# A rotary embedding kernel: the first row of slab 1 moved to ScalarE's DMA ring at the start

## The chip, the cores and the metric

The kernel runs on one core of a Trainium2 chip. The metric is the device time of one execution in microseconds (us), smaller being better. The five engines of the core run their own instruction streams: TensorE (PE), VectorE (DVE), ScalarE (ACT), GpSimd (POOL) and SyncE (SP). Data moves between the main memory and the on-chip memory by 16 DMA engines. A DMA is issued by SyncE, ScalarE or GpSimd, each into a ring of its own, and the 16 DMA engines serve all the rings.

## The reference

Rotary position embedding, in float32, over x of shape (16, 512, 1024), seen as 16 heads of 64. The two halves of each head are rotated by the cosine and sine of the position:

```python
x = x.reshape(batch, seq, num_heads, head_dim)
x1, x2 = x[..., :half_dim], x[..., half_dim:]
cos = cos[None, :, None, :]
sin = sin[None, :, None, :]
rotated = np.concatenate([
    x1 * cos - x2 * sin,
    x1 * sin + x2 * cos
], axis=-1)
```

The output has 16 x 512 x 16 x 64 float32 values: 33.55 MB are read and 33.55 MB written.

## The kernel before

The input is cut into 8 slabs (`nslabs`) of two batches each. A slab is a tile of 128 partitions x 8192 float32 (`W`), 4 MB: each partition holds 8 rows (`rpp`) of 1024 elements (`dim`), which lie side by side in the main memory, so that one partition is one run of 32 KB. There are five slots for slabs (`slots`), and a slab is written back from the slot it was loaded into.

Loads are issued by SyncE, one DMA for each slab (`load`, L60 to L62). Load 0 is the first DMA. Then GpSimd issues the loads of the cosine and the sine table (L73, into `raw`). Loads 1 to 4 carry a dependency written out by hand on the cosine table (L80): SyncE issues them once that table has landed. Loads 5, 6 and 7 are issued inside the loop (L150) and wait until the store of the slab that held their slot has landed.

The tables are spread to all rows by GpSimd (L89 to L98, a selection matrix `pick` and a bf16 copy of the tables) and eight small matmuls (L104), and VectorE copies the result into `tab` (L110). This happens once.

The work on the slabs goes in passes. The first slab and the last two are done in two passes of four rows each, the others in one pass of eight. For each pass ScalarE casts the slab to bf16 (`cast`, L119, into `xb`), VectorE does two multiplications (L140) and one addition (L143), and ScalarE casts the result back into the slab (L146). After the last pass of a slab ScalarE issues the store (L148). ScalarE's program order is: the cast of pass 0, then for each pass the cast of the next pass, the copy back of this pass, and the store. So the stores and all work of ScalarE stand in one program order, and before the change the first DMA that ScalarE issues is the store of slab 0.

Of the kernel before, what the change touches and what calls it, by code (L numbers as in the profile page):

```python
# [2 lines left out]

# [4 lines left out]


@with_exitstack  # L10
def kernel(
    ctx: ExitStack,
    tc: tile.TileContext,
    x: bass.AP,
    cos: bass.AP,
    sin: bass.AP,
    num_heads: int,
    out: bass.AP,
):
    nc = tc.nc  # L20
    P = nc.NUM_PARTITIONS

    batch, seq, dim = x.shape
    nh = num_heads
    hd = dim // nh
    half = hd // 2
    bf16 = mybir.dt.bfloat16
    f32 = mybir.dt.float32

    nb = 2  # L30
    slots = 5
    nslabs = batch // nb
    rpp = nb * seq // P
    W = rpp * dim
    SP = seq // rpp
    TW = rpp * half

    out_flat = out.rearrange("b s h d -> b s (h d)")

    singles = ctx.enter_context(tc.tile_pool(name="singles", bufs=1))  # L40
    slabs = ctx.enter_context(tc.tile_pool(name="slabs", bufs=slots))
    xpool = ctx.enter_context(tc.tile_pool(name="xpool", bufs=2))
    psum = ctx.enter_context(tc.tile_pool(
        name="psum", bufs=1, space=bass.MemoryType.PSUM))


    def dram(t, s, a=0, n=W):
        return bass.AP(tensor=t.tensor, offset=t.offset + s * nb * seq * dim + a,
                       ap=[[W, P], [1, n]])


    def view(t, offset, *dims):
        return dataclasses.replace(t, offset=t.offset + offset,
                                   ap=[t.ap[0], *[list(d) for d in dims]])


    slab = {}


    def load(s):  # L60
        slab[s] = slabs.tile([P, W], f32, tag="slab", name="slab")
        return nc.sync.dma_start(out=slab[s], in_=dram(x, s))  # L62


    load(0)


    TR = seq // P
    G = rpp // TR
    table = {}  # L70
    raw = singles.tile([P, 2 * TR * half], f32, tag="raw")
    for i, src in enumerate((cos, sin)):
        table[i] = nc.gpsimd.dma_start(out=view(raw, i * TR * half, (1, TR * half)), in_=bass.AP(  # L73
            tensor=src.tensor, offset=src.offset,
            ap=[[TR * half, P], [1, TR * half]]))

    for s in range(1, slots):
        tc.add_manual_dep(  # L80
            load(s).ins, table[0].ins.name,
            mybir.DependencyInfo(mybir.DependencyClass.Sync,
                                 mybir.DependencyReason.DATA),
            reason="issue")

    pick = singles.tile([P, 2 * G * P], bf16, tag="pick")
    nc.gpsimd.memset(pick, 0.0)  # L89
    for g in range(2 * G):  # L90
        part = view(pick, g * P, (SP, P // SP), (1, SP))
        nc.gpsimd.affine_select(  # L92
            out=part, in_=part, compare_op=mybir.AluOpType.not_equal,
            fill=1.0 if g < G else -1.0, base=-(g % G),
            pattern=[[0, P // SP], [-G, SP]], channel_multiplier=1)

    tab1 = singles.tile([P, 2 * TR * half], bf16, tag="tab1")
    nc.gpsimd.tensor_copy(out=tab1, in_=raw)  # L98

    acc = psum.tile([P, 2 * rpp * hd], f32, tag="acc")  # L100
    for i in range(2):
        for h in range(2):
            for g in range(G):
                nc.tensor.matmul(  # L104
                    view(acc, (i * rpp + g * TR) * hd + h * half, (hd, TR), (1, half)),
                    view(pick, (i * h * G + g) * P, (1, P)),
                    view(tab1, i * TR * half, (half, TR), (1, half)),
                    start=True, stop=True)
    tab = singles.tile([P, 2 * rpp * hd], bf16, tag="tab")
    nc.vector.tensor_copy(out=tab, in_=acc)  # L110

    xb = {}


    def cast(u):
        s, r, n = u
        if r == 0:
            xb[s] = xpool.tile([P, W], bf16, tag="xb", name="xb")
        nc.scalar.copy(out=view(xb[s], r * dim, (1, n * dim)),  # L119
                       in_=view(slab[s], r * dim, (1, n * dim)))  # L120

    passes = []
    for s in range(nslabs):
        n = rpp if 1 <= s < nslabs - 2 else rpp // 2
        passes += [(s, r, n) for r in range(0, rpp, n)]


    cast(passes[0])
    for i, (s, r, n) in enumerate(passes):
        if i + 1 < len(passes):
            cast(passes[i + 1])
        xs = view(slab[s], r * dim, (1, n * dim))
        xu = view(xb[s], r * dim, (1, n * dim))

        t2 = view(slab[s].bitcast(bf16), 2 * r * dim, (1, n * dim))
        for t, a in ((t2, rpp * hd), (xu, 0)):
            nc.vector.tensor_mul(  # L140
                out=t, in0=xu,
                in1=view(tab, a + r * hd, (hd, n), (0, nh), (1, hd)))
        nc.vector.tensor_add(  # L143
            out=xu, in0=xu, in1=view(t2, half, (hd, n * nh), (-half, 2), (1, half)))

        nc.scalar.copy(out=xs, in_=xu)  # L146
        if r + n == rpp:
            nc.scalar.dma_start(out=dram(out_flat, s), in_=slab[s])  # L148
            if s + slots < nslabs:
                load(s + slots)  # L150


# [1 line left out]
_INS = ['x', 'cos', 'sin', 'num_heads']  # L154
_OUTS = [((16, 512, 16, 64), 'float32')]

_NUMBERS = {'num_heads': 16}


# [26 lines left out]
```

## Time and profile before

| What | Value |
|---|---|
| Median of 4 runs | 162.28 us (162.18 to 162.3) |
| The profiled execution: its time | 162.27 us |
| The profiled execution: its span, first to last instruction | 160.5 us |
| ScalarE busy | 113.5 us (71%) |
| VectorE busy | 108.5 us (68%) |
| Data moved | 67.24 MB, 419 GB/s over the span |
| Issue of load 0 (SyncE) | 0.74 us |
| Cosine and sine table, issue to landing | 7.2 and 9.1 us |
| First cast (slab 0) / cast of slab 1 start | 13.50 / 23.20 us |
| First store issued (ScalarE) | 37.26 us |
| Last store issued (ScalarE) | 144.66 us |

The table reads in order of time: the span counts from the first instruction, and the time of the execution holds 1.8 us around it. In the views, L140 is line 140 of the kernel, `slab<-xb` is a tile that is written and what is read for it, and ACTq or SPq is the queue of an engine that issues DMAs. A DMA ring appears as q1 (SyncE's), q10 (ScalarE's) and q0 (GpSimd's). The granted clock was 1.0 in the whole execution.

### The profile page before, as it was taken

To read this page: it belongs to the slowest core of one execution; us is meant where nothing else is said; L and a number is where in the kernel's file an instruction comes from. 1 tells how busy PE (TensorE), PEld (TensorE's weight loads), DVE (VectorE), ACT (ScalarE), POOL (GpSimd) and SP (SyncE) were. 2 spreads that over 40 slices of the span, in tenths; PEclk is the share of its full clock that TensorE was granted. 3 is DMA by queue.
4 is the path that set the end of the run, shared out by engine and by line. 5 is a ranking of instruction groups with operands and counts; after the bars stand their busy time and mean duration, and the time that the engine had idled before them with its cause. 6 is when DMAs were issued, how large, how long until landed. Compare 5 with 4: busy or idle time off the path is not lost.

```text
span 160.5 us, 169 instructions
## 1 busy us (share of the span) xinstructions
PE 1.0 (1%) x8; PEld 0.8 (1%) x8; DVE 108.5 (68%) x34; ACT 113.5 (71%) x23; POOL 3.4 (2%) x12
## 2 busy tenths in 40 slices
PE   0011000000000000000000000000000000000000
PEld 0010000000000000000000000000000000000000
DVE  0003799999989979997996199939559599910000
ACT  3006939998998999899909995099995999280000
POOL 7000000000000000000000000000000000000000
DMA  7999999999999999999999999999999999999994
GB/s 245 425 408 392 465 449 392 441 474 392 351 433 400 465 441 392 474 441 392 474 441 392 449 449 408 425 465 416 416 457 433 400 466 441 392 474 441 392 474 180
DMA packets 2368, 67.24 MB, mean 419 GB/s; under 512 B 288, under 2 KB 288, under 8 KB 320
## 3 DMA queue, kind: packets, MB, share of 16 engines
q1 hardware_dynamic: 1152, 33.55, 49.5%
q10 hardware_dynamic: 1152, 33.55, 48.4%
q0 software_dynamic: 64, 0.13, 0.2%
HBM read 33.69 MB, written 33.55 MB: 419 GB/s over the span
## 4 chain that ended last, share of the span: by engine, by line
DMA 49%; ACT 30%; issue 6%; DVE 4%; ACTq 0%; SPq 0%; POOLq 0%
DMA slab<-in_x_dram 24%; DMA out_dram<-slab 21%; ACT slab L146 16%; ACT xb L119 14%; DMA raw<-in_cos_dram 4%; DVE slab L140 1%; DVE xb L140 1%; DVE xb L143 1%; ACTq L148 0%; SPq L62 0%; ACTq L146 0%; POOLq L167 0%
## 5 line engine op out<-in xcount | busy, mean ns | idle before, releaser
L119 ACT CAST xb<-slab 128x4096 bf16<-128x4096 f32 (+1 forms) x11 | 56.6, 5155 | 26.9 <-DMA slab<-in_x_dram 25.6
L146 ACT CAST slab<-xb 128x4096 f32<-128x4096 bf16 (+1 forms) x11 | 56.6, 5153 | 3.5 <-DVE xb L143 3.5
L140 DVE TENSOR_TENSOR slab<-xb,tab 128x4096 bf16<-128x4096 bf16 (+1 forms) x11 | 35.9, 3260 | 19.1 <-ACT xb L119 19.0
L143 DVE TENSOR_TENSOR xb<-xb,slab 128x4096 bf16<-128x4096 bf16 (+1 forms) x11 | 35.9, 3261 | 0.3
L140 DVE TENSOR_TENSOR xb<-xb,tab 128x4096 bf16<-128x4096 bf16 (+1 forms) x11 | 35.9, 3261 | 0.3
L110 DVE CAST tab<-acc 128x1024 bf16<-128x1024 f32 x1 | 1.2, 1225 | 12.7 <-PE acc L104 12.7
L119 ACT ACT_TABLE_LOAD x1 | 1.3, 1283 | 0.7 <-PEq L167 0.7
L104 PE MATMUL acc<-tab,pick 128*128 128x128 bf16 x8 | 1.0, 305 | 11.6 <-POOL tab L98 11.6
L92 POOL TENSOR_SCALAR_AFFINE_SELECT pick<-pick 128x128 bf16<-128x128 bf16 x4 | 1.0, 288 | 0.1
L104 PEld LDWEIGHTS <-pick 128*128 128x128 bf16 x8 | 0.8, 136 | 11.5 <-issue 8.1
L73 POOL DMA_DIRECT2D raw<-in_cos_dram x1 | 0.7, 674 | 0.8 <-POOLq L167 0.8
L98 POOL CAST tab<-raw 128x256 bf16<-128x256 f32 x1 | 0.4, 396 | 7.1 <-DMA raw<-in_sin_dram 7.1
L89 POOL MEMSET pick<- 128x512 bf16 x1 | 0.5, 543 | 0.0
L73 POOL DMA_DIRECT2D raw<-in_sin_dram x1 | 0.5, 534 | 0.0
L167 POOL MEMSET const-float32-0.0<- 128x1 f32 x1 | 0.1, 98 | 0.2 <-issue 0.2
L167 POOL MEMSET const-bfloat16-1.0<- 128x1 bf16 x1 | 0.1, 102 | 0.0
L167 POOL MEMSET const-uint8-127<- 128x1 uint8 x1 | 0.1, 101 | 0.0
L167 POOL MEMSET const-float32-1.0<- 128x1 f32 x1 | 0.1, 99 | 0.0
## 6 DMA issues: line engine op xcount, KB each, us to landing
slab<-in_x_dram SPq DMA_DIRECT2D x8, 4096.0 KB, 24.1
out_dram<-slab ACTq DMA_DIRECT2D x8, 4096.0 KB, 26.9
raw<-in_cos_dram POOLq DMA_DIRECT2D x1, 64.0 KB, 7.2
raw<-in_sin_dram POOLq DMA_DIRECT2D x1, 64.0 KB, 9.1
```

The lines of the kernel that those rows point to most:

```text
L73: table[i] = nc.gpsimd.dma_start(out=view(raw, i * TR * half, (1, TR * half)), in_=bass.AP(tensor=src.tensor, offset=src.offset, ap=[[TR * ...
L89: nc.gpsimd.memset(pick, 0.0)
L92: nc.gpsimd.affine_select(out=part, in_=part, compare_op=mybir.AluOpType.not_equal, fill=1.0 if g < G else -1.0, base=-(g % G), pattern=[[ ...
L98: nc.gpsimd.tensor_copy(out=tab1, in_=raw)
L104: nc.tensor.matmul(view(acc, (i * rpp + g * TR) * hd + h * half, (hd, TR), (1, half)), view(pick, (i * h * G + g) * P, (1, P)), view(tab1, ...
L110: nc.vector.tensor_copy(out=tab, in_=acc)
L119: nc.scalar.copy(out=view(xb[s], r * dim, (1, n * dim)), in_=view(slab[s], r * dim, (1, n * dim)))
L140: nc.vector.tensor_mul(out=t, in0=xu, in1=view(tab, a + r * hd, (hd, n), (0, nh), (1, hd)))
L143: nc.vector.tensor_add(out=xu, in0=xu, in1=view(t2, half, (hd, n * nh), (-half, 2), (1, half)))
L146: nc.scalar.copy(out=xs, in_=xu)
L167: nc = _bacc.Bacc("TRN2", target_bir_lowering=False, num_devices=1)
```

## The change

The slot of slab 1 is taken at the start. Of each of its partitions, the first row (`early` = 1024 elements, 4 KB, 512 KB in all) is loaded by a DMA that ScalarE issues, its first instruction. When SyncE comes to load 1, it loads the remaining 7 rows of each partition (28 KB), still after the cosine table. The other loads, the tables, the work and the stores are the same. The cast of slab 1 waits for both of the slab's transfers.

```diff
+    early = dim
...
     def load(s):
+        if s == 1:
+            return nc.sync.dma_start(out=view(slab[s], early, (1, W - early)),
+                                     in_=dram(x, s, early, W - early))
         slab[s] = slabs.tile([P, W], f32, tag="slab", name="slab")
         return nc.sync.dma_start(out=slab[s], in_=dram(x, s))


     load(0)
+    slab[1] = slabs.tile([P, W], f32, tag="slab", name="slab")
+    nc.scalar.dma_start(out=view(slab[1], 0, (1, early)), in_=dram(x, 1, 0, early))
```

## The prediction

> **What bounds the kernel now.** I read the shares and the slices of the page first, then the DMA queues, the chain of waits, and last the view by windows, which prices what the slices only hint at.
>
> ```profile
> PE 1.0 (1%) x8; PEld 0.8 (1%) x8; DVE 108.5 (68%) x34; ACT 113.5 (71%) x23; POOL 3.4 (2%) x12
> ...
> DMA  7999999999999999999999999999999999999994
> GB/s 245 425 408 392 465 449 392 441 474 392 351 433 400 465 441 392 474 441 392 474 441 392 449 449 408 425 465 416 416 457 433 400 466 441 392 474 441 392 474 180
> ...
> q1 hardware_dynamic: 1152, 33.55, 49.5%
> q10 hardware_dynamic: 1152, 33.55, 48.4%
> q0 software_dynamic: 64, 0.13, 0.2%
> ```
>
> No compute engine is full, while the DMA engines are at 9 in every slice but the first and the last. q1 is SyncE's ring (loads), q10 ScalarE's (stores), q0 GpSimd's (the two tables). The chain of waits agrees, because its long pieces are transfers that wait for each other:
>
> ```profile
> 52.03 7.02 ACT xb L119
> 59.05 6.93 ACT slab L146
> 65.98 0.02 issue
> 66.00 33.07 DMA out_dram<-slab
> 99.07 0.02 SPq L62
> 99.09 0.03 issue
> 99.12 24.20 DMA slab<-in_x_dram
> ```
>
> A 4 MB transfer that took 24 to 33 us was queueing: 4.19 MB at the full rate of about 433 GB/s is 9.7 us. So I ask at what moments the DMA engines were not delivering. The view by windows, in steps of 12 us (columns: window, length, busy time of PE, PEld, DVE, ACT and POOL, clock, DMA share, GB/s):
>
> ```profile
> 1.70:13.70 12.00, 1.01 (x8) 0.84 (x8) 1.03 (x1) 0.51 (x2) 2.70 (x8) 1.00 1.01 410
> 13.70:25.70 12.00, 0.00 (x0) 0.00 (x0) 8.72 (x5) 9.41 (x3) 0.00 (x0) 1.00 1.00 431
> 25.70:37.70 12.00, 0.00 (x0) 0.00 (x0) 11.93 (x5) 11.55 (x4) 0.00 (x0) 1.00 1.01 437
> 37.70:49.70 12.00, 0.00 (x0) 0.00 (x0) 11.14 (x4) 12.00 (x2) 0.00 (x0) 1.00 0.99 396
> 49.70:61.70 12.00, 0.00 (x0) 0.00 (x0) 10.96 (x3) 11.59 (x3) 0.00 (x0) 1.00 1.01 434
> 61.70:121.70 60.00, 0.00 (x0) 0.00 (x0) 47.69 (x14) 49.68 (x9) 0.00 (x0) 1.00 1.01 436
> 121.70:157.70 36.00, 0.00 (x0) 0.00 (x0) 17.02 (x8) 17.82 (x5) 0.00 (x0) 1.00 1.00 433
> ```
>
> Two windows fall short although the engines are busy in them (share 1.01 and 0.99): the first, with 410 GB/s, and the one that begins with the first store, with 396. A window counts a packet where it starts, which blurs these by a packet per engine; the trace's packet records are sharper. A 32 KB packet takes 1.213 us nearly everywhere. At the start all 16 first packets begin between 1.74 and 2.80 us and end only between 3.64 and 4.22; by 4.00 us 570 KB have moved where (4.00 - 1.74) x 432 would be 976 KB, so 0.94 us of the whole DMA is lost. Between 39 and 44 us load packets stretch to 1.4 to 2.1 us, two of them on most engines, and 391 KB are missing: 0.90 us. That is 1.5 us after the first store is issued, which is also the first time that ScalarE's ring is used:
>
> ```profile
> 37.26 0.38 ACTq L148 DMA_DIRECT2D out_dram<-slab  x1
> ```
>
> No later store and no later load shows a stretched packet. The sum closes: 1.74 us before the first packet, 0.94, 0.90, 67.24 MB at 432.7 GB/s = 155.4 us, together 159.0; the last store's last packet ends at 159.3, and 1.2 us of closing barriers make the span of 160.5. The reader is to see that the time is bytes over a fixed rate plus two losses of about 0.9 us, and that only these losses are to be had.
>
> **What the Trainium skill says.** "DMA: Bandwidth & Descriptors", Issuing engines are not separate DMA queues: DMAs from different engines share the same 16 DMA engines, and issuing from several saves only issue time. The windows agree: one ring alone makes 433 GB/s (from 121.7 us), two together 434. That page's Queues, rings and completion order: an engine takes turns between rings packet by packet. The records agree: every engine puts one 4 KB table packet between two 32 KB load packets near 6.1 to 6.6 us. "Perfetto Trace Analysis", DMA Instruction — HWDGE (DVE, Sync): the descriptor generator is locked for one DMA at a time; no two issues overlap in this trace, so it shows nothing of that. I found no page on what the first use of a ring costs.
>
> **The change, part by part.** *Bytes.* They stay. Of slab 1's 128 rows of 32 KB, each is cut into 4 KB and 28 KB. A 4 KB packet took 0.159 us (tables), a 32 KB one 1.213, so 28 KB is estimated at 1.213 - 4096 x (1.213 - 0.159) / 28672 = 1.062 us. The two make 1.221, 0.008 more; 8 per engine, plus one more semaphore packet (0.009), is 0.07 us of DMA, all on the bound.
>
> *The issue on ScalarE.* One more DMA issue, 0.34 to 0.38 us by L148's row, ahead of the table load at 0.73. ScalarE then idles from 2.0 to 13.5, so it costs nothing; that wait is cover of 11.5 us. If the generator serves one at a time and ScalarE wins, load 0 is issued some 0.35 us later, but then ScalarE's own packets occupy the engines. Nothing on POOL moves. SP waits for the cosine table ahead of load 1 as before.
>
> *Load 0 lands later.* Taking turns, each engine does eight 4 KB packets within load 0's eight: 8 x 0.159 + 0.009 = 1.28 us, so the cast at 13.50 starts near 14.8. The cosine table is behind at most five of them (0.8 us), so loads 1 to 4 are issued from about 9.2 instead of 8.4, while SyncE's ring has work until 14.3. The sine table is at most 1.3 us later, and the full table is ready at 15.2 instead of 13.9, before the first cast ends at 18.4.
>
> *Slab 1.* The same bytes stand ahead of its end: it lands 0.07 us later than 23.2. ScalarE reaches it earlier (14.8 + 7.1 = 21.9), so ScalarE stays anchored there. VectorE, without a gap from 17.14 to 43.94, shifts by 1.28 to 45.2; ScalarE's slab 1 copy (44.60) must wait for it, so store 1 goes out 0.6 us later, at 52.3. It then queues anyway: by the packet records store 0 ends at 61.2. At the end the last store is issued at 144.66 and the one ahead of it lands at 149.6, so 4.9 us of delay there are free. The added wait, ScalarE's slab 1 cast on the new transfer too, is for one that lands at about 13.
>
> *The two losses.* This decides. The trace of before doesn't show a first use of ScalarE's ring apart from a first store. Bounds for the stall at 39 to 44 us: it goes wholly (-0.90) or stays (0). Bounds for the start: the small packets fill the ramp (-0.94, as 512 KB are enough to fill 406 KB), or a second start-up adds to it (+0.9, the size of the first). I take -0.90 and 0: the two losses are of one size, each comes with the first use of a hardware ring, and neither comes back when a ring picks up new work. After the change both rings are started in the same microsecond while no packet has anything to lose, so the start-ups lie beside each other. I don't take the ramp as filled, since the engines' first packets all end together however early they began, which looks like one delay common to all requests.
>
> Sum against the profiled execution (162.27 us, of which the span is 160.5; the median is 162.28): 162.27 - 0.90 + 0.07 = 161.44, put at 161.45.
>
> **The rivals.** *B, the stall belongs to the store.* It is the first write to the output as much as the first use of the ring, or a ring that wakes beside a busy one; ScalarE's ring would be idle again from about 13 to 37 us. For it: GpSimd's ring starts at 6.1 us without a stretched packet. Against: that ring is of the software kind, with packets too small to show much. It gives 162.27 + 0.07 = 162.34. That is also what it comes to if the change doesn't do what it says and no ring is made ready.
>
> *C, both losses go.* The small packets also use part of the ramp: 0.4 to 0.9 us less than the forecast, 160.55 to 161.05. For it: the ramp's gap. Against: the common end of the first packets.
>
> *D, slower.* The start of ScalarE's ring stretches load 0's packets as it stretched load 3's, after SyncE's own start-up instead of beside it, and the store's stall stays because it is the store's. Price up to 0.90 + 0.07: 163.24; with half of it beside the ramp, 162.8. It decides once more than 0.25 us of additional loss stands in the first 13 us while the window from 37.7 still shows about 396 GB/s. For it: the stretched packets at 39 us were those of the other ring. Slab 0's delay alone isn't this case, for its 1.28 us meet 4.9 us of slack.
>
> **How the numbers follow.** About 0.2% (0.32 us) is what a measurement can tell from no change. Forecast 0.49, with a range of its own of 161.1 to 161.8; B 0.25; C 0.06; D 0.20. The first and C are faster (0.55), B the same, D slower. The range 160.9 to 162.7 takes in the forecast and B whole (0.74), half of C, and the small end of D, some 0.8.
>
> **What would show it.** Right: the 12 us after the first store carry about 430 GB/s instead of 396, no load packet near 40 us is stretched, the first window stays near 410, the cast of slab 0 starts near 14.8, and load 7 lands 0.8 us before 123.3. Wrong: a window from 37.7 that stays near 396 (B), or first packets of load 0 that end later than 4.3 us on top of it (D). A cast of slab 0 still at 13.5 would refute the turns taken packet by packet.

## The result, and the profile after

The change makes the kernel slightly slower: 162.37 us median (41 runs) against 162.16 us for the kernel before in the same measurements (61 runs), a ratio of 1.0013 with a 95% interval of 1.0009 to 1.0018, that is 0.21 us (0.15 to 0.29). The forecast was 161.45 us. All ratios here compare fast executions alone: a few, one of these 41 among them, ran in a slower state and are left out. The profiled execution took 162.21 us with a span of 160.4; it is the fastest of the 41, and that of before, with 162.27, lies in the slower half of its own runs. So the two spans show no loss, and the 0.21 us has to be found in a piece that repeats from run to run.

The page of the kernel after, slices and queues:

```profile
DMA  6999999999999999999999999999999999999993
GB/s 216 394 435 457 400 483 392 458 458 392 392 392 400 515 392 392 515 400 392 482 433 392 482 433 392 441 474 392 408 507 392 400 507 400 392 515 400 392 482 172
...
q10 hardware_dynamic: 1296, 34.08, 49.2%
q1 hardware_dynamic: 1152, 33.03, 48.6%
```

The change does what it says: ScalarE's ring (q10) carries 0.52 MB and 144 packets more (128 of data, 16 for the semaphore), and the DMA engines are as full as before. The view by windows, with the columns of the prediction:

```profile
1.70:13.70 12.00, 1.01 (x8) 0.84 (x8) 0.16 (x1) 0.75 (x1) 2.70 (x8) 1.00 1.00 403
13.70:25.70 12.00, 0.00 (x0) 0.00 (x0) 8.40 (x5) 9.56 (x3) 0.00 (x0) 1.00 1.02 438
25.70:37.70 12.00, 0.00 (x0) 0.00 (x0) 11.93 (x5) 11.59 (x3) 0.00 (x0) 1.00 1.01 437
37.70:49.70 12.00, 0.00 (x0) 0.00 (x0) 11.93 (x4) 11.55 (x2) 0.00 (x0) 1.00 0.98 396
49.70:61.70 12.00, 0.00 (x0) 0.00 (x0) 10.70 (x3) 11.59 (x3) 0.00 (x0) 1.00 1.01 434
```

The fourth line is the one that the forecast hung on. It was to rise to about 430 GB/s and stands at 396, as before. The stall at the first store is still there, although ScalarE's ring had carried its first transfer from 3.55 to 14.22 us. The timeline of ScalarE (start, length, what) shows that the rest went as worked out:

```profile
0.74 0.40 ACTq L73 DMA_DIRECT2D slab<-in_x_dram  x1
1.17 1.28 ACT L127 ACT_TABLE_LOAD   x1 [1.17 <-PEq L175]
14.70 7.11 ACT L127 CAST xb<-slab 128x4096 bf16<-128x4096 f32 x2 [12.24 <-DMA slab<-in_x_dram]
23.25 7.02 ACT L127 CAST xb<-slab 128x8192 bf16<-128x8192 f32 x1 [1.45 <-DMA slab<-in_x_dram]
...
45.17 7.02 ACT L154 CAST slab<-xb 128x8192 f32<-128x8192 bf16 x1 [0.45 <-DVE xb L151]
52.22 0.34 ACTq L156 DMA_DIRECT2D out_dram<-slab  x1
```

Slab 0 is cast at 14.70, slab 1 at 23.25, slab 1's copy back at 45.17 and store 1 goes out at 52.22; the prediction had 14.8, 23.3, 45.2 and 52.3.

What repeats from run to run is at the very end. SyncE closes the program with a row of waits for the semaphores of all DMAs. Its waits in the kernel before (engine and line, what it waited for: us in total, times, longest):

```profile
SPq L181 <- DMA out_dram<-slab: 36.0, 4, 9.6
SPq L181 <- DMA slab<-in_x_dram: 23.9, 1, 23.9
```

and in the kernel after:

```profile
SPq L189 <- DMA out_dram<-slab: 55.6, 1, 55.6
SPq L189 <- DMA slab<-in_x_dram: 4.5, 1, 4.5
```

Before, SyncE waits for the last four stores one after another, and the last one comes last. After, the one wait of 55.6 us is by the trace a wait for two semaphores, that of load 7, which lands at 123.04 us, and that of the last store, which comes last; SyncE has the other waits still ahead of it when the store has landed. By the records, one wait and a drain follow the last packet before (at 159.63 and 159.70, the packet having ended at 159.27); after, four waits at 159.39, 159.45, 159.51 and 159.57 and then the drain at 159.64 (packet end 158.99). From the last packet to the end of the span it is 1.22 us before and 1.45 after: 0.23 us, the size of the loss, and 0.18 of it are three more waits of about 0.06 us each. In the traces the DMAs of SyncE and ScalarE take eight semaphores in turn, so a 17th transfer moves the last store on to another one.

### The profile page after: what moved, and what is told of

It reads as the page before. It is cut to its first block, busy times and chain, and to the rows that moved or that the text cites. A ratio compares the mean times of both kernels' runs of the same rounds, so it can differ in the third digit from the quotient of the medians.

```text
span 160.4 us, 172 instructions
## 1 busy us (share of the span) xinstructions
PE 1.0 (1%) x8; PEld 0.8 (1%) x8; DVE 108.4 (68%) x34; ACT 113.6 (71%) x23; POOL 3.4 (2%) x12
## 3 DMA queue, kind: packets, MB, share of 16 engines
q1 hardware_dynamic: 1152, 33.03, 48.6%
## 4 chain that ended last, share of the span: by engine, by line
DMA 44%; ACT 23%; DVE 20%; issue 3%; ACTq 0%; SPq 0%
DMA slab<-in_x_dram 24%; DMA out_dram<-slab 20%; ACT slab L154 13%; ACT xb L127 10%; DVE xb L148 7%; DVE slab L148 7%; DVE xb L151 6%; ACTq L156 0%; SPq L68 0%; ACTq L154 0%
```

## The experiments

Twelve runs were made, one of them of the change itself, each timed against the kernel before on the same chip. The table gathers what the packet records say of each. "Stall" is the time that the DMA engines lost at the first bulk store, against 432.7 GB/s, the full rate of the prediction's sum (37 to 46 us; for the four rows and store 0 on SyncE 46 to 60); "close" goes from the last packet to the end of the span; "transfers" are those on the two hardware rings.

| Kernel | Transfers | Stall us | Close us | Ratio to before (95%) |
|---|---|---|---|---|
| before | 16 | 0.93 | 1.22 | 1 |
| the change | 17 | 0.76 | 1.45 | 1.0013 (1.0009 to 1.0018) |
| the change again | 17 | 0.82 | 1.44 | 1.0010 (1.0002 to 1.0018) |
| cut on SyncE | 17 | 0.70 | 1.46 | 1.0031 (1.0012 to 1.0050) |
| store 0 on SyncE | 16 | 0.82 | 1.22 | 1.0234 (1.0199 to 1.0270) |
| small store first | 17 | 0.78 | 1.44 | 1.0032 (1.0020 to 1.0044) |
| four rows | 17 | 0.66 | 1.43 | 1.0012 (1.0004 to 1.0020) |
| one tiny load | 17 | 0.93 | 1.44 | 1.0012 (1.0006 to 1.0019) |
| eight tiny loads | 24 | 1.08 | 1.22 | 1.0211 (1.0194 to 1.0227) |
| row store first | 17 | 0.85 | 1.46 | 1.0092 (1.0078 to 1.0105) |
| row on GpSimd | 16 | 0.60 | 1.23 | 0.9999 (0.9983 to 1.0015) |
| store 0 in 4 KB, joined | 16 | 0.68 | 1.22 | 0.9996 (0.9988 to 1.0004) |
| store 0 in 16 KB, joined | 16 | 0.92 | 1.22 | 1.0001 (0.9993 to 1.0009) |
| store 0 in 8 KB | 17 | 0.24 | 1.55 | 1.0049 (1.0035 to 1.0063) |

Each stall is read from one execution; among kernels whose first bulk store is of 32 KB packets it spreads from 0.60 to 1.08 us, so the 0.76 of the change is no gain.

### What the stall is: store 0 through SyncE's ring

```diff
-            nc.scalar.dma_start(out=dram(out_flat, s), in_=slab[s])
+            (nc.sync if s == 0 else nc.scalar).dma_start(out=dram(out_flat, s), in_=slab[s])
```

> The kernel before, but store 0 goes through SyncE's ring behind load 4, so that it starts near 51 us in a ring that is already moving packets; ScalarE's ring then starts with store 1 at about 52 us. Theory S (the stall belongs to the first store, whichever ring): packets are stretched near 51 us, when store 0 begins, and none when ScalarE's ring starts after it. Theory W (the stall is a ring that starts beside a busy one): no stretched packet when SyncE's ring goes over from loads to store 0, but about 0.9 us lost within 3 us of store 1's issue. In both, the window from 37.7 to 49.7 carries about 432 GB/s instead of 396, and the time stays within 0.3 us of before, since the stall is only moved.

The issues in this kernel's timeline:

```profile
37.27 0.34 SPq L148 DMA_DIRECT2D out_dram<-slab  x1
...
51.24 0.37 ACTq L148 DMA_DIRECT2D out_dram<-slab  x1
```

and its windows:

```profile
37.70:49.70 12.00, 0.00 (x0) 0.00 (x0) 11.54 (x4) 12.00 (x2) 0.00 (x0) 1.00 1.02 437
49.70:61.70 12.00, 0.00 (x0) 0.00 (x0) 10.93 (x3) 11.56 (x3) 0.00 (x0) 1.00 0.99 399
```

The store is issued at the same 37.27 us, but the stretch after it is now whole (437), and the loss has moved to where SyncE's ring goes over from loads to this store (399). By the packet records the stretched packets are load 4's last ones, from 48.8 to 52.6 us, and the first store packet starts at 52.0 (in the kernel before, 39.1 and 41.1 us): the loads stretch 2 to 3 us ahead of the first recorded store packet. ScalarE's ring carries its first packet of the whole program at 55.6 us, with no stretched packet near it. So the stall belongs to the stores, and the first use of a ring costs nothing that these records show. Theory S held, W fell. The time missed its expectation: the kernel is 3.8 us slower. The loads of the last three slabs land 5 to 12 us later than before, and between 123 and 155 us, while the last slabs are still being worked on, 4.3 us of DMA are lost, about the size of the loss.

### Does an early store take it away?

```diff
     load(0)
+    junk = singles.tile([P, 128], f32, tag="junk")
+    nc.vector.memset(junk, 0.0)
+    nc.scalar.dma_start(out=dram(out_flat, nslabs - 1, 0, 128), in_=junk)
```

> The kernel before, with a store of 512 bytes of each partition (64 KB of zeros, to rows that the last store overwrites) as ScalarE's first DMA at the start. Theory S1 (what stalls is the first write to the output or the first store of ScalarE's ring): the stall near 40 us goes, the window from 37.7 us rises from 396 to about 430 GB/s, and the time falls by 0.5 to 0.8 us. Theory W (a ring that starts again beside a busy one, after any idle time): the window stays near 396, the time is 0.1 to 0.3 us above before.

The stall stayed at 0.78 us and the time rose by 0.53 us. The close accounts for 0.22 of it and the added 64 KB, at the full rate, for 0.15; the rest isn't located, since the profiled execution is the fastest of the six and only 0.2 us over that of before. The second trial stored whole rows (`[P, dim]` in place of `[P, 128]`):

> The kernel before with a store of 4 KB of each partition (512 KB of zeros, in 4 KB packets, to rows that the last store overwrites) as ScalarE's first DMA. The 512 KB alone cost 1.28 us of DMA, the close 0.2. Theory S2 (the stall is a matter of the first store of some size, and comes once): the stall near 40 us falls from 0.9 to below 0.3 us, the window from 37.7 to 49.7 rises to 420 GB/s or more, and the time is 0.6 to 0.9 us over before. Theory S3 (the stall comes each time that stores set in after a stretch of loads alone): it stays at 0.7 to 0.9 us, the window near 396 to 404, and the time is 1.3 to 1.6 us over before.

```profile
37.70:49.70 12.00, 0.00 (x0) 0.00 (x0) 10.90 (x3) 11.59 (x3) 0.00 (x0) 1.00 1.01 404
```

A stall of 0.85 us, and 1.5 us over before, as S3 had it (1.21 for the 512 KB at the full rate, 0.24 at the close). An earlier store of 512 KB through the same ring doesn't take the stall away. But that early store has no stall of its own, which S3 in its wide form would ask for: its 4 KB packets set in at 6.05 us beside load 0, after 4 us of loads alone, and only 0.03 us are lost between 4.5 and 13 us, as before. So an onset of stores is not enough by itself; the size of the packets or the longer stretch of loads ahead must come in.

### Is it the size of the store's packets?

```diff
+                piece = dim          # 4 * dim in the second kernel
...
+                                ap=[[W, P], [piece, W // piece], [1, piece]]),
+                    in_=view(slab[s], 0, (piece, W // piece), (1, piece)))
```

> The kernel before with store 0 written as eight pieces of 4 KB for each partition in one DMA, no transfer added. Theory P (the stall at the first store comes from 32 KB packets taken in while the load packets are still under way): the stall of 0.8 to 0.9 us falls below 0.3 us; the small packets cost an estimated 8 x (8 x 0.159 - 1.213) = 0.47 us, so the time is between 0.2 us under and 0.1 us over before. Theory S3 (any onset of stores after loads alone costs it): the stall stays, the time is 0.4 to 0.6 us over before.

> The same with two pieces of 16 KB. Theory P: the stall falls to about half (0.4 to 0.5 us), the packets cost about 0.06 us, so the time is 0.3 to 0.4 us under before. Theory S3: stall and time as before, at most 0.1 us over.

Neither tested anything. In both profiles ScalarE's ring still has 1152 packets, the 1024 of data all of 32 KB: pieces that lie side by side had been joined before the chip ran, for the DMA instruction in the trace already names runs of 32 KB. What they give is a repeat of the kernel before, with ratios of 0.9996 and 1.0001. The last run separates the pieces by force:

```diff
+                c = 2 * dim
+                for a in (0, c):
+                    nc.scalar.dma_start(
+                        out=bass.AP(tensor=out_flat.tensor, offset=out_flat.offset + a,
+                                    ap=[[W, P], [2 * c, 2], [1, c]]),
+                        in_=view(slab[s], a, (2 * c, 2), (1, c)))
```

> The kernel before with store 0 as two DMAs, of the even and of the odd 8 KB pieces of each partition, so that the pieces can't be joined and its packets are of 8 KB. Theory P (the stall at the first store comes from its 32 KB packets): the stall of 0.6 to 0.9 us falls below 0.3 us; the packets cost about 0.2 us, the 17th transfer 0.2 at the close, so the time is 0.1 to 0.4 us under before. Theory S3 (any onset of stores after loads alone costs it, whatever the packets): the stall stays at 0.6 to 0.9 us and the time is 0.3 to 0.5 us over before.

```profile
37.70:49.70 12.00, 0.00 (x0) 0.00 (x0) 10.27 (x3) 11.15 (x2) 0.00 (x0) 1.00 0.98 415
```

The stall fell to 0.24 us, which speaks for P, but weakly: counted from 37 to 60 us the loss is 0.44 us, not far below the 0.57 of the row on GpSimd, and store 0 is now two transfers, so the packets are not all that changed. The time is 0.8 us over before, which neither theory had. In its records 0.22 us more are lost than before from 46 to 60 us, 0.35 more from 60 to 123 and 0.36 more after 155, and the close takes 0.33 more. So in this one profile the loss is smaller with small packets, and more than its saving is paid elsewhere. What happens inside the DMA engines when stores set in stays open.

### What the extra 0.2 us is

First suspect was the cut into 4 and 28 KB. The cut alone, both parts in SyncE's ring at load 1's place:

```diff
+            first = nc.sync.dma_start(out=view(slab[1], 0, (1, early)),
+                                      in_=dram(x, 1, 0, early))
...
-    nc.scalar.dma_start(out=view(slab[1], 0, (1, early)), in_=dram(x, 1, 0, early))
```

> Slab 1's load is cut into 4 KB and 28 KB as in the change, but both parts go through SyncE's ring at load 1's place, after the cosine table. Theory T1 (the extra 0.2 us is the price of smaller packets and one more transfer): slower than before by 0.07 to 0.2 us, about as the change. Theory T2 (the extra is paid for the second ring at the start: the issue beside load 0, slab 0's later landing): no more than 0.07 us slower than before. Both: slab 0 lands at 13.0 us as before, and the stall at the first store stays near 396 GB/s from 37.7 us.

By the medians it costs 0.25 us, about what the change costs, so the second ring is not needed for the loss; three of its runs, at 164.2 to 164.3 us, make the interval too wide to say more. Slab 0 landed at 12.84 us in it, so slab 0's delay is not needed either. The other end, four rows instead of one:

```diff
-    early = dim
+    early = 4 * dim
```

> The change with four rows of each partition (16 KB, 2 MB in all) through ScalarE's ring at the start instead of one. Theory T1 (price of packets): the cut rows are 16 and 16 KB, as many packets as in the change, so it costs what the change does, 0.1 to 0.25 us over before. Theory T3 (the price is slab 0's delay): slab 0 lands near 17.9 us instead of 14.2, the compute of slabs 0 to 2 runs some 4 us later, and the loss grows to 0.5 us or more. Theory W: the stall after the first store stays at about 396 GB/s wherever that store now falls.

Slab 0 lands at 17.6 us, the stall moves with the first store to after 45 us, and the time is that of the change (1.0012). A delay of slab 0 by 4.6 us is therefore covered: T3 fell. T1 as "the price of packets" was still alive, but the closes in the table had by then split into 1.22 for 16 transfers and about 1.44 for 17, whatever the extra transfer was. This can be tried without any cut:

```diff
     load(0)
+    for j in range(1):          # 8 in the second kernel
+        tiny = singles.tile([16, 16], f32, tag=f"tiny{j}", name=f"tiny{j}")
+        nc.scalar.dma_start(out=tiny, in_=bass.AP(
+            tensor=x.tensor, offset=x.offset, ap=[[16, 16], [1, 16]]))
```

> The kernel before plus one load of 1 KB (16 partitions of 64 bytes) through ScalarE's ring at the start, which nothing reads; no slab is cut. Theory C (the extra is paid at the close: with 17 transfers instead of 16 on the hardware rings, the last store's semaphore is waited for earlier in SyncE's closing row of waits, and three more waits follow it): the closing stretch from the last packet to the end of the span grows from 1.22 to 1.44 us, and the time is 0.15 to 0.25 us over before. Theory T1 (price of the cut packets): nothing is cut here, so within 0.05 us of before.

> The change itself, on the same chip as the three others. 0.13 to 0.3 us over before. Theory C: a closing stretch of 1.44 us, and 0.0 to 0.1 us over the kernel with one tiny load, that rest being the price of the cut packets (estimated at 0.07 us).

One load of 1 KB, which nothing reads, costs 0.19 us (0.10 to 0.31): as much as the change on the same chip (162.34 against 162.33 us). Its closing waits:

```profile
SPq L186 <- DMA out_dram<-slab: 55.6, 1, 55.6
SPq L186 <- DMA slab<-in_x_dram: 4.5, 1, 4.5
```

are those of the change. Theory C held; the price of packets can't explain it.

> The same with eight such tiny loads, 24 transfers in all, so that the last store comes to the same semaphore (of eight that are used in turn) as before. Theory C: the closing stretch is back at 1.22 us and the time within 0.1 us of before, below that of the kernel with one tiny load, although there are seven more transfers. Theory N (each added transfer costs something by its number): eight cost more than one, 0.5 us or more over before.

```profile
SPq L186 <- DMA out_dram<-slab: 36.0, 4, 9.6
SPq L186 <- DMA slab<-in_x_dram: 23.9, 1, 23.9
SPq L62 <- DMA slab<-in_x_dram: 12.7, 1, 12.7
```

The close came back to 1.22 us with 24 transfers, as expected, and the order of waits to that of before. The time did not: 3.5 us over before. The third line gives the reason, and it is a side effect of the edit: the eight semaphores had been used up, so load 1 had to wait 12.7 us for load 0, an earlier transfer on the same semaphore, the DMA engines ran dry, and 2.7 us were lost between 13 and 37 us. As a test of the time this run is spoilt; as a test of the close it is clean. The clean test of the time keeps the early row but takes it out of the count:

```diff
-    nc.scalar.dma_start(out=view(slab[1], 0, (1, early)), in_=dram(x, 1, 0, early))
...
+    nc.gpsimd.dma_start(out=view(slab[1], 0, (1, early)), in_=dram(x, 1, 0, early))
```

> The change with the early row issued by GpSimd behind the two tables instead of by ScalarE: the same cut rows and the same early bytes, but 16 transfers on the two hardware rings as before. Theory C (the close is what costs): the closing stretch is 1.22 to 1.30 us, and the time is 0.0 to 0.12 us over before (0.07 of it the cut packets). Theory T1 (the cut itself costs): 0.15 us or more over before, as the change.

```profile
SPq L190 <- DMA out_dram<-slab: 36.1, 4, 9.6
SPq L190 <- DMA slab<-in_x_dram: 23.8, 1, 23.8
```

The same cut rows, the close at 1.23 us, and no loss (0.9999). Its interval reaches to 1.0015, because of one execution at 163.65 us (the other eleven lie between 161.87 and 162.39), so this run alone does not exclude the change's loss; together with the tiny load, which has the loss without the cut, it does place it.

## Why the prediction was wrong, point by point

**The step that failed** is the one under "The two losses": "I take -0.90 and 0". It read the stall at 39 us as the first use of ScalarE's ring, on the grounds that both losses were of one size and came with the first use of a hardware ring. In the trace of before, first use of the ring and first store are the same event, and the text said so; it then chose. Measured: the ring was in use from 3.55 to 14.22 us and the stall stayed at 0.76 and 0.82 us in two profiles; with store 0 in the other ring the stall went with the store. The value to take was 0. The counter-evidence stood in the records of before: GpSimd's ring had started at 6.1 us without a stretched packet, and the prediction set it aside.

**The other bound taken was right:** the ramp of the start isn't filled. ScalarE's first packet comes at 3.55 us, when SyncE's first packets are done, and 0.89 us are lost before 4.5 us against 0.95 in the kernel before. The two issues at 0.74 us did not delay load 0 either: its first packet starts at 1.74 us in both kernels.

**The price of the cut,** 0.07 us, fits where it can be seen: between 4.5 and 37 us the records of the change lose 0.13 us against 0.07 in the kernel before. The timings don't resolve it.

**A term was missing:** the close, +0.23 us. The prediction took the 1.2 us after the last packet as fixed. Rival B, which keeps the stall, had the stall right and missed only this; 0.07 and 0.23 make 0.30, just above the measured 0.15 to 0.29. That its 162.34 us stand so near the measured 162.37 is luck: it started from 162.27, and the median of before in the same measurements is 162.16.

**Slab 0's delay** is covered, as stated: 1.28 us were expected, slab 0's cast moved by 1.20, and four rows with a delay of 4.6 us cost no more. Turns are taken packet by packet as the Trainium skill has it ("DMA: Bandwidth & Descriptors", Queues, rings and completion order): in the records of the change each engine puts one 4 KB packet between two of 32 KB until ScalarE's transfer ends at 14.22 us.

**Rival D** did not occur: in the first 13 us the DMA engines lost 0.97 us, as in the kernel before. That the first window shows 403 GB/s and not the 410 named as a sign is no loss, then: a window counts a packet where it starts. Load 7's last packet ends 0.29 us earlier (122.68 against 122.97), not 0.8.

No version beat the kernel before by more than the noise. Those that tie with it are the row on GpSimd and the two repeats.

## What to carry to other kernels

When two things happen for the first time at the same moment, the trace that shows them together can't say which one costs; a forecast should then weigh what the trace shows of each alone, such as another ring that starts without a stall. In a kernel that is bound by DMA, sum the time lost against the full rate and take the close as a part of that sum: here the order of the closing waits depends on how many transfers there are. A transfer added to save a fraction of a microsecond can cost 0.2 us there without one byte more.

## What the runs showed of the hardware that was not expected

- A bulk store that set in after loads alone cost 0.60 to 1.08 us of all 16 DMA engines when store and loads were of 32 KB packets, after an early 512 KB store too (0.85 us), and 0.24 us (0.44 counted to 60 us) in one profile with an 8 KB first store. The early store of 4 KB packets itself cost no such time. The later change from loads and stores to stores alone, near 123 us, costs nothing in the records (433 GB/s).
- The close differs by 0.23 us with the semaphore on which the last store falls: 1.22 to 1.23 us with 16 or 24 transfers, 1.43 to 1.55 with 17. A wait that is already met takes about 0.06 us.
- The first use of ScalarE's ring, at 3.55 us with small loads or at 55.6 us beside a busy ring, stretched no packet.
